# Where the operands of the products lie in SBUF: pads in the tiles and pools of a two-layer trunk

## The chip, the cores and the metric

The kernel runs on 1 core of one Trainium2 chip. The metric is the device time of one execution in microseconds (us). The time before is 1105.18 us, the median of 3 runs (1104.79 to 1105.24).

## What is computed

A trunk of two layers over 512 tokens of 1024 channels, float32. Cut to what matters here:

```
for l in range(2):
    u = rms_norm(h, norm1_g[l]);  proj = u @ w_in[l]              # 1024 x 2576
    mix = concat(pool_mixer(...), diff_attention(...), gla_mixer(...))   # each from slices of proj
    h = h + mix @ w_out[l]                                        # 1024 x 1024
    z = rms_norm(h, norm2_g[l])
    h = h + square(relu(z @ w_mlp1[l])) @ w_mlp2[l]               # 1024 x 4096, 4096 x 1024
return rms_norm(h, final_norm_g)
```

Nearly all of the arithmetic is in these products of matrices.

## The kernel before

Channels lie on the 128 partitions and tokens along the free side. Each large product is made from three products of float32r: both factors are split into a high and a low part (ScalarE casts the high part, VectorE subtracts it to leave the low part; `split`, L118), and high x high, high x low and low x high are added up in one PSUM bank (`mm3`, L138; the page shows them as lines L139 to L141). One such part is one instruction on TensorE, called a product below: it loads 128x128 stationary weights (the page's PEld) and streams the moving operand past them, 512 or 256 columns of 128 partitions (the page's PE).

The order in which names stand in the page: in `psm<-sh,wh` the moving operand is `sh`, the weights are `wh`, and the result goes to `psm`. The stages, each once per layer, in order of time:

- **Projections** (`project`, L330): 512-column products with the normed input `uh`, `ul` moving and a cut weight tile `wh`, `wl` stationary. They are filled in between the steps of the attention and of the gated linear attention (GLA), whose products are small.
- **Values** (`bytoken`, L341): 384 products of 256 columns over both layers, lines L349 to L351. Here the cut weight tile moves and `uh`, `ul` are stationary. GLA's own values are 192 products of 272 columns through the same lines.
- **Output projection** (`output`, L578): 512-column products with `yh`, `yl` or `y` moving.
- **Plain half of the first MLP** (`plain`, L822): 192 products of 512 columns, `zh`, `zl` moving.
- **Seven products** (`seven`, L901): the rest of the first MLP, 28 blocks over both layers by Strassen's scheme with seven smaller products, 84 instructions of 256 columns each, 2352 in all (lines L913 to L915). The moving operand is a quarter of `zh`, `zl` or one of the sums `th1` to `th4`, `tl1` to `tl4`; the weights are `wh`, `wl` (the tile from `cut`) or the sums `bh`, `bl`, `ch`, `cl`, `dh`, `dl` that `prepare` (L881) makes.
- **Second MLP** (`second`, L1003): 1488 products of 512 columns, `sh`, `sl` moving and `wh`, `wl` stationary, and 96 of 256 columns at the very end. Four quarters per layer; each quarter is one stage of seven products and then one of second products.

TensorE's order is the program's own (`manual_schedule`). Weights come by DMA from SyncE's queue, two raw tiles deep, cut tiles three deep. All tiles live in pools (`tile_pool`) that lie one behind the other in SBUF: first `cst`, `res` (h, uh, ul, zh, zl), `wp` (raw, wh, wl), `sm`, and behind these per layer either `at` and `a2` (the attention) or `mp` and `sp` (the MLP). The size of each tile decides where the next one starts. Read from the built program, the places where operands begin, as the start address modulo 128 bytes, are these before and after the change:

| products | columns, count | moving / weights before | apart | moving / weights after | apart |
|---|---|---|---|---|---|
| projections, plain half (`uh` or `zh` with `wh`) | 512, 864 | 32 / 32 | 0 | 32 / 32 | 0 |
| second MLP (`sh` with `wh`) | 512, 1488 | 96 / 32 | 64 | 32 / 32 | 0 |
| seven: `zh` with `wh` | 256, 336 | 32 / 32 | 0 | 32 / 96 | 64 |
| seven: `th1`, `th2`, `th3` with `bh`, `ch` | 256, 1008 | 96 / 96 | 0 | 32 / 96 | 64 |
| seven: `zh` with `ch`, `dh` | 256, 672 | 32 / 96 | 64 | 32 / 96 | 64 |
| seven: `th4` with `wh` | 256, 336 | 96 / 32 | 64 | 32 / 96 | 64 |
| values (`wh` moving, `uh` stationary) | 256, 384 | 32 / 32 | 0 | 96 / 32 | 64 |
| GLA's values, first and third 272 columns of a tile | 272, 120 | 32 / 32 | 0 | 96 / 32 | 64 |
| GLA's values, second 272 columns of a tile | 272, 72 | 96 / 32 | 64 | 32 / 32 | 0 |
| output, `yh` with `wh` or with a spare tile `wx` | 512, 240 | 96 / 32 or 96 | 64 or 0 | 96 / 32 | 64 |
| output, `y` with `wh` or with a spare tile `wx` | 512, 144 | 0 or 96 / 32 or 96 | 0 to 96 | 32 / 32 | 0 |

The low parts lie as the high ones do. The small float32 products of the attention and of GLA (572 of the 6472 instructions) move too; three kinds of transposes among them, with the constants `cn` moving, have their operands 32 (L480), 96 (L519) and 0 bytes (L676) apart before. On VectorE, all operands of `wl<-raw,wh` begin at 32, while in `s<-raw,raw` (L888) they begin at 96, 32 and 96. A step from one 128-column slice of a tile to the next is 512 bytes, so all slices of a tile have its place, but for the 272 columns.

Of the kernel before, what the change touches and what calls it, by code (L numbers as in the profile page):

```python
# [8 lines left out]
F32 = mybir.dt.float32  # L9
F32R = mybir.dt.float32r  # L10
# [6 lines left out]
P = 128  # L17
# [3 lines left out]
KT = D // P  # L21
# [5 lines left out]
NCH = T // CHUNK  # L27
# [6 lines left out]
PLAIN = 2  # L34
HT = T // 2
W = 16 + T
BIG = 1.0e30

LEAD = [(0, 0), (1, 0), (2, 0), (3, 0), (0, 1), (1, 1), (2, 1), (3, 1), (4, 0), (5, 0), (6, 0), (7, 0), (4, 1), (5, 1), (6, 1), (7, 1)]
# [32 lines left out]
def trunk(ctx: ExitStack, tc: tile.TileContext, xt, wfm, wdv, wgv, wout, wm1, wm2, poolw, wg2, par, con, msk, out, outt):  # L72
# [5 lines left out]
    wp = ctx.enter_context(tc.tile_pool(name="wp", bufs=3))  # L78
# [6 lines left out]
    def load(src, n=1024):  # L85
        raw = wp.tile([P, 1024], F32, name="raw", bufs=2)[:, 0:n]
        nc.sync.dma_start(out=raw, in_=src)
        return raw
# [36 lines left out]
            nc.vector.scalar_tensor_tensor(out=dst_l, in0=src, scalar=scale, in1=dst_h.bitcast(F32),  # L125
                                           op0=ALU.mult, op1=ALU.subtract)

    def cut(raw):
        n = raw.shape[1]
        wh = wp.tile([P, 1024], F32R, name="wh")[:, 0:n]  # L130
        wl = wp.tile([P, 1024], F32R, name="wl")[:, 0:n]
        split(wh, wl, raw)
        return wh, wl

    def weights(src, n=1024):
        return cut(load(src, n))

    def mm3(ps, sh, sl, mh, ml, first, last):  # L138
        nc.tensor.matmul(ps, sh, mh, start=first, stop=False)  # L139
# [98 lines left out]
    for l in range(L):  # L238
# [4 lines left out]
        lead = []  # L243
# [3 lines left out]
        for k in range(KT):  # L247
            for i, m, a, b in LOADS if l == 0 else ():
                if i == k:
                    if a == 0:  # L250
                        lead.append([wp.tile([P, 1024], F32R, name=n) for n in ("wh", "wl")])
                    split(lead[m][0][:, a:b], lead[m][1][:, a:b], first[m][:, a:b])
            split(uh[k], ul[k], h[k], g1[k])
        if l == 0:
# [5 lines left out]
        with ExitStack() as ph:  # L260
            at = ph.enter_context(tc.tile_pool(name=f"at{l}", bufs=1))
# [4 lines left out]
            def mixed(k):  # L266

                if yh[k] is None:
                    y = at.tile([P, 2, T], F32R, name="y", tag=f"Y{k}")
                    yh[k], yl[k] = y[:, 0], y[:, 1]  # L270
                return yh[k], yl[k]

            def tmp(name):
                return a2.tile([P, W], F32, name=name, tag="w", bufs=4)[:, 0:T]
# [7 lines left out]
            def advance():  # L282

                n = sum(len(j["src"]) for j in live)
                for j in todo:
                    if j["w"] is None and j["into"]:
                        if "w" + j["name"][1:] in held:
                            break
                        wh, wl = j["into"]()
                        split(wh, wl, load(j["src"][0]))  # L290
                        j["w"] = [(wh, wl)]
                    elif j["w"] is None:
                        n += len(j["src"])
                        if n > 3:
                            break
                        j["w"] = [weights(x, x.shape[1]) for x in j["src"]]
                        live.append(j)

            def run(j):
# [298 lines left out]
            for x in ORDER:  # L598
                if x in ("v0", "v1"):
                    n = int(x[1])  # L600
# [55 lines left out]
            nc.scalar.activation(ed, ed, AF.Exp)  # L656
            nc.scalar.activation(en, bc, AF.Exp, scale=-1.0)
            nc.scalar.activation(ep, bc, AF.Exp)
            dec = at.tile([P, NCH], F32, name="dec")
            nc.scalar.activation(dec, bc3[:, :, CHUNK - 1], AF.Exp)  # L660
            nc.vector.tensor_tensor(out=ed, in0=kd, in1=ed, op=ALU.mult)
            nc.vector.tensor_tensor(out=ki, in0=kd, in1=en, op=ALU.mult)
# [19 lines left out]
            for half in range(2):  # L682
                n = 4 - half
# [21 lines left out]
            po = pc.tile([P, NT, 256], F32, name="pog", tag="pc")  # L705
            for t in range(NT):
# [7 lines left out]
                for j in range(2):  # L714
                    c = 2 * t + j
# [49 lines left out]
            for u in range(nu):  # L765
                f = SF[u]
# [47 lines left out]
        with ExitStack() as ph:  # L814
            mp = ph.enter_context(tc.tile_pool(name=f"mp{l}", bufs=2))
            byhand = ExitStack()
            byhand.enter_context(tc.manual_schedule(engines={mybir.EngineType.PE}))
            fast = ExitStack()
            sp = fast.enter_context(tc.tile_pool(name=f"sp{l}", bufs=1))
            acts, tz = {}, {}  # L820

            def plain(u, j):  # L822
# [58 lines left out]
            def prepare(u):  # L881

                raw1 = load(wm1[l, u, 0])
                raw2 = sp.tile([P, 1024], F32, name="raw2", bufs=2)
                nc.sync.dma_start(out=raw2, in_=wm1[l, u, 1])
                a = cut(raw1)
                s13 = sp.tile([P, 2, 512], F32, name="s13")
                nc.vector.tensor_tensor(out=s13, in0=raw1.rearrange("p (a b) -> p a b", a=2),  # L888
                                        in1=raw2[:, 0:512].unsqueeze(1).broadcast_to([P, 2, 512]), op=ALU.add)
                b = [sp.tile([P, 2, 512], F32R, name=f"b{n}", bufs=2) for n in "hl"]  # L890
                split(*b, s13)
                s24 = sp.tile([P, 2, 512], F32, name="s24")
                nc.vector.tensor_add(s24[:, 0], s13[:, 1], raw1[:, 0:512])
                nc.vector.tensor_add(s24[:, 1], s24[:, 0], raw2[:, 512:1024])
                c = [sp.tile([P, 2, 512], F32R, name=f"c{n}") for n in "hl"]
                split(*c, s24)
                d = [sp.tile([P, 512], F32R, name=f"d{n}", bufs=2) for n in "hl"]
                split(*d, raw2[:, 512:1024])
                return a, b, c, d

# [64 lines left out]
            w, late = None, None  # L965
            for q in range(QT):
                for u in range(q * UQ, (q + 1) * UQ):
                    if u == 0:
# [10 lines left out]
                        w = prepare(PLAIN)  # L979
# [11 lines left out]
                    if not final:  # L991
                        w = prepare(u + 1)
# [22 lines left out]
                lead = []  # L1015
# [18 lines left out]
                        w = prepare((q + 1) * UQ)  # L1034
                byhand.close()
                if ends:
                    w2t = [weights(wm2[l, q, m]) for m in range(KT - 2, KT)]
                    ph.enter_context(tc.manual_schedule(engines={mybir.EngineType.DVE}))
                    for half in range(2):
                        n = slice(half * HT, (half + 1) * HT)  # L1040
# [90 lines left out]
```

## Time and profile before

| | |
|---|---|
| median of 3 runs | 1105.18 us |
| the profiled execution | 1104.88 us |
| its span on the core | 1103.1 us |
| TensorE busy | 1091.8 us (99%), 6472 instructions |
| VectorE busy | 746.9 us (68%) |
| ScalarE busy | 577.4 us (52%) |
| mean granted TensorE clock | 0.996 |

The span runs from the first to the last instruction of the core; 1.8 us of the execution's time lie outside it. A matmul's row in the timeline has a start and a busy time. The busy times of neighbours overlap, since TensorE takes the next product before the last has drained, so what one product costs in a stream is the distance from its start to the next one's start, called pitch below. It is had from the starts of two products and the number between them.

### The profile page before, as it was taken

To read this page: it belongs to the slowest core of one execution; us is meant where nothing else is said; L and a number is where in the kernel's file an instruction comes from. 1 tells how busy PE (TensorE), PEld (TensorE's weight loads), DVE (VectorE), ACT (ScalarE), POOL (GpSimd) and SP (SyncE) were. 2 spreads that over 40 slices of the span, in tenths; PEclk is the share of its full clock that TensorE was granted. 3 is DMA by queue.
4 is the path that set the end of the run, shared out by engine and by line. 5 is a ranking of instruction groups with operands and counts; after the bars stand their busy time and mean duration, and the time that the engine had idled before them with its cause. 6 is when DMAs were issued, how large, how long until landed. Compare 5 with 4: busy or idle time off the path is not lost.

```text
span 1103.1 us, 16249 instructions
## 1 busy us (share of the span) xinstructions
PE 1091.8 (99%) x6472; PEld 963.2 (87%) x6472; DVE 746.9 (68%) x1115; ACT 577.4 (52%) x998; POOL 47.3 (4%) x84
## 2 busy tenths in 40 slices
PE   9999999999999999999999999999999999999997
PEld 7888898888898898898887988887989989989986
DVE  6587873996676676675637688749866666666654
ACT  6526773774265265265434377648733733733742
POOL 3101000000000000000021110000000000000000
PEclk9999999999999999999999999999999999999999
DMA  6322111432322323312222121214232232332222
GB/s 212 96 67 71 64 58 58 154 115 96 115 97 96 115 96 96 115 59 79 91 79 73 61 86 58 93 43 154 93 115 92 100 115 83 109 115 79 76 77 77
DMA packets 32224, 102.76 MB, mean 93 GB/s; under 512 B 3698, under 2 KB 5524, under 8 KB 32148
## 3 DMA queue, kind: packets, MB, share of 16 engines
q1 hardware_dynamic: 31716, 101.17, 28.2%
q8 instruction: 51, 0.84, 0.3%
q10 hardware_dynamic: 432, 0.55, 0.1%
q14 instruction: 25, 0.20, 0.1%
HBM read 99.61 MB, written 2.10 MB: 92 GB/s over the span
## 4 chain that ended last, share of the span: by engine, by line
PE 96%; issue 1%; DVE 1%; DMA 1%; ACT 0%; SPq 0%; POOLq 0%; DVEq 0%; POOL 0%; ACTq 0%
PE psm L141 18%; PE psm L140 18%; PE psm L139 18%; PE psx L913 5%; PE psx L915 5%; PE psx L914 5%; PE psz L915 2%; PE psz L913 2%; PE psz L914 2%; PE psm L349 2%; PE psm L350 2%; PE psm L351 2%; PE po L492 1%; PE psy L913 1%; PE psy L915 1%; PE psy L914 1%
## 5 line engine op out<-in xcount | busy, mean ns | idle before, releaser
L121 ACT CAST wh<-raw 128x1024 fp32r<-128x1024 f32 (+2 forms) x155 | 160.0, 1034 | 292.4 <-PE psm L140 209.7
L122 DVE TENSOR_TENSOR wl<-raw,wh 128x1024 fp32r<-128x1024 f32 (+2 forms) x155 | 185.9, 1201 | 74.2 <-ACT wh L121 73.8
L141 PE MATMUL psm<-sh,wl 128*128 128x512 f32 (+1 forms) x528 | 204.6, 387 | 0.0
L140 PE MATMUL psm<-sl,wh 128*128 128x512 f32 (+1 forms) x528 | 203.3, 385 | 0.0
L139 PE MATMUL psm<-sh,wh 128*128 128x512 f32 (+1 forms) x528 | 201.6, 382 | 0.0
L1011 DVE TENSOR_TENSOR tm<-psm,rb 128x512 f32<-128x512 f32 (+1 forms) x66 | 44.5, 674 | 114.5 <-PE psm L141 114.5
L140 PEld LDWEIGHTS psm<-sl,wh 128*128 128x128 f32 x528 | 99.2, 188 | 21.4
L139 PEld LDWEIGHTS psm<-sh,wh 128*128 128x128 f32 x528 | 99.2, 188 | 20.5
L141 PEld LDWEIGHTS psm<-sh,wl 128*128 128x128 f32 x528 | 99.4, 188 | 18.5
L139 PE MATMUL psm<-uh,wh 128*128 128x512 f32 x224 | 94.8, 423 | 1.4 <-ACT uh L124 1.4
L140 PE MATMUL psm<-ul,wh 128*128 128x512 f32 x224 | 88.5, 395 | 0.3 <-DVE ul L125 0.3
L141 PE MATMUL psm<-uh,wl 128*128 128x512 f32 x224 | 88.6, 396 | 0.1
L349 PE MATMUL psm<-wh,uh 128*128 128x256 f32 (+1 forms) x192 | 56.6, 295 | 0.0
L351 PE MATMUL psm<-wh,ul 128*128 128x256 f32 (+1 forms) x192 | 54.7, 285 | 0.0
L350 PE MATMUL psm<-wl,uh 128*128 128x256 f32 (+1 forms) x192 | 54.7, 285 | 0.0
L141 PEld LDWEIGHTS psm<-uh,wl 128*128 128x128 f32 x224 | 42.5, 190 | 10.4 <-DVE wl L122 1.0
L139 PEld LDWEIGHTS psm<-uh,wh 128*128 128x128 f32 x224 | 42.7, 190 | 10.1 <-ACT uh L124 1.8
L140 PEld LDWEIGHTS psm<-ul,wh 128*128 128x128 f32 x224 | 42.7, 191 | 9.1 <-issue 1.0
L462 ACT ACTIVATE pp<-psc,mn,nrt 128x128 f32<-128x128 f32 (+3 forms) x64 | 39.0, 613 | 13.9 <-DVE mn L459 12.0
L1012 DVE TENSOR_TENSOR h<-h,tm 128x512 f32<-128x512 f32 (+1 forms) x66 | 44.5, 674 | 1.5
L122 DVE TENSOR_TENSOR sl<-o,sh 128x1024 fp32r<-128x1024 f32 (+1 forms) x36 | 35.0, 987 | 11.2 <-ACT sh L121 11.2
L888 DVE TENSOR_TENSOR s<-raw,raw 128x1024 f32<-128x1024 f32 x28 | 34.2, 1222 | 5.8 <-DMA raw<-in_wm 5.5
(381 smaller groups left out, 2727.3 us busy)
## 6 DMA issues: line engine op xcount, KB each, us to landing
raw<-in_wm SPq DMA_DIRECT2D x120, 512.0 KB, 3.5
raw<-in_wfm SPq DMA_DIRECT2D x27, 512.0 KB, 3.5
raw<-in_wout SPq DMA_DIRECT2D x16, 512.0 KB, 3.5
raw<-in_wdv SPq DMA_DIRECT2D x8, 512.0 KB, 3.5
raw<-in_wm SPq DMA_DIRECT2D x16, 256.0 KB, 4.0
h<-in_xt SPq DMA_DIRECT2D x8, 256.0 KB, 5.2
raw<-in_wgv SPq DMA_DIRECT2D x4, 408.0 KB, 3.2
out<-o SPq DMA_DIRECT2D x8, 128.0 KB, 1.8
```

Of the source, the lines that this page charges most:

```text
L121: nc.scalar.copy(out=dst_h, in_=src)
L122: nc.vector.tensor_sub(dst_l, src, dst_h.bitcast(F32))
L139: nc.tensor.matmul(ps, sh, mh, start=first, stop=False)
L140: nc.tensor.matmul(ps, sh, ml, start=False, stop=False)
L141: nc.tensor.matmul(ps, sl, mh, start=False, stop=last)
L349: nc.tensor.matmul(ps, uh[k][:, ts], wh[:, s], start=k == 0, stop=False)
L350: nc.tensor.matmul(ps, uh[k][:, ts], wl[:, s], start=False, stop=False)
L351: nc.tensor.matmul(ps, ul[k][:, ts], wh[:, s], start=False, stop=k == KT - 1)
L913: nc.tensor.matmul(ps, sh[:, s], mh, start=first and k == 0, stop=False, skip_group_check=True)
L914: nc.tensor.matmul(ps, sh[:, s], ml, start=False, stop=False, skip_group_check=True)
L915: nc.tensor.matmul(ps, sl[:, s], mh, start=False, stop=k == 3, skip_group_check=True)
L1011: nc.vector.tensor_tensor(out=tm, in0=ps, in1=r2[:, n], op=ALU.mult)
```

## The change

Tiles and pools get pads. The tiles that hold cut weights are 32 floats (`PAD`, 128 bytes) longer, so that their own places stay, and a view of 16 floats (`HP`, 64 bytes) further in is used where the weights serve 256-column products: `wh`, `wl` in the seven products and the last MLP weights, `b`, `c` and `d`, and the moving weights of the values. An unused tile of 64 bytes at the head of the pool `mp` and one in `at` move all that lies behind them by 64 bytes, and `dec` takes 128 bytes instead of 32. The built programs of before and after have the same instructions in the same order on every engine, with the same waits and the same values waited for; the addresses alone differ.

```diff
+PAD = 32
+HP = PAD // 2
...
-    def cut(raw):
+    def cut(raw, at=0):
         n = raw.shape[1]
-        wh = wp.tile([P, 1024], F32R, name="wh")[:, 0:n]
-        wl = wp.tile([P, 1024], F32R, name="wl")[:, 0:n]
+        wh = wp.tile([P, 1024 + PAD], F32R, name="wh")[:, at:at + n]
+        wl = wp.tile([P, 1024 + PAD], F32R, name="wl")[:, at:at + n]
         split(wh, wl, raw)
         return wh, wl
-    def weights(src, n=1024):
-        return cut(load(src, n))
+    def weights(src, n=1024, at=0):
+        return cut(load(src, n), at)
...
-                        lead.append([wp.tile([P, 1024], F32R, name=n) for n in ("wh", "wl")])
+                        lead.append([wp.tile([P, 1024 + PAD], F32R, name=n)[:, 0:1024] for n in ("wh", "wl")])
...
+            at.tile([P, HP], F32, name="gap")
...
-                        j["w"] = [weights(x, x.shape[1]) for x in j["src"]]
+                        j["w"] = [weights(x, x.shape[1], 0 if j["name"][0] in "po" else HP) for x in j["src"]]
...
-            dec = at.tile([P, NCH], F32, name="dec")
+            dec = at.tile([P, PAD], F32, name="dec")[:, 0:NCH]
...
+            mp.tile([P, HP], F32, name="gap", bufs=1)
...
-                a = cut(raw1)
+                a = cut(raw1, HP)
...
-                b = [sp.tile([P, 2, 512], F32R, name=f"b{n}", bufs=2) for n in "hl"]
+                b = [sp.tile([P, 1024 + PAD], F32R, name=f"b{n}", bufs=2)[:, HP:HP + 1024].rearrange("p (a n) -> p a n", a=2) for n in "hl"]
...
-                c = [sp.tile([P, 2, 512], F32R, name=f"c{n}") for n in "hl"]
+                c = [sp.tile([P, 1024 + PAD], F32R, name=f"c{n}")[:, HP:HP + 1024].rearrange("p (a n) -> p a n", a=2) for n in "hl"]
...
-                d = [sp.tile([P, 512], F32R, name=f"d{n}", bufs=2) for n in "hl"]
+                d = [sp.tile([P, 512 + PAD], F32R, name=f"d{n}", bufs=2)[:, HP:HP + 512] for n in "hl"]
...
-                    w2t = [weights(wm2[l, q, m]) for m in range(KT - 2, KT)]
+                    w2t = [weights(wm2[l, q, m], at=HP) for m in range(KT - 2, KT)]
```

## Rows read from the trace of the kernel before

**Rows 1.** The page: busy time of the engines, and the chain that ended last.
```profile
PE 1091.8 (99%) x6472; PEld 963.2 (87%) x6472; DVE 746.9 (68%) x1115; ACT 577.4 (52%) x998; POOL 47.3 (4%) x84
...
PE 96%; issue 1%; DVE 1%; DMA 1%; ACT 0%; SPq 0%; POOLq 0%; DVEq 0%; POOL 0%; ACTq 0%
```

**Rows 2.** Waits of TensorE: us in total, times, longest; its longest two.
```profile
PE psm L139 <- ACT uh L124: 1.4, 1, 1.4
PE early L112 <- DVE ones L109: 1.0, 1, 1.0
```

**Rows 3.** Windows: stretch, its length, busy us of each engine, clock, DMA share, GB/s.
```profile
256.00:299.70 43.70, 43.70 (x194) 35.88 (x193) 28.93 (x35) 14.23 (x17) 0.00 (x0) 1.00 0.36 116
299.70:339.20 39.50, 39.50 (x338) 39.42 (x337) 26.41 (x34) 25.68 (x41) 0.00 (x0) 1.00 0.25 86
...
76.00:90.00 14.00, 14.00 (x115) 13.85 (x114) 8.51 (x17) 3.52 (x6) 2.91 (x1) 1.00 0.14 39
90.00:158.00 68.00, 68.00 (x398) 59.50 (x397) 56.66 (x121) 53.22 (x127) 4.10 (x6) 1.00 0.22 70
```

**Rows 4.** Timeline of TensorE: start, busy us; first of each run of twelve products.
```profile
311.21 0.28 PE L913 MATMUL psx<-th,wh 128*128 128x256 f32 x1
...
312.57 0.28 PE L913 MATMUL psx<-th,ch 128*128 128x256 f32 x1
...
314.01 0.29 PE L913 MATMUL psy<-zh,dh 128*128 128x256 f32 x1
...
315.39 0.28 PE L913 MATMUL psz<-zh,ch 128*128 128x256 f32 x1
...
316.75 0.28 PE L913 MATMUL psx<-th,bh 128*128 128x256 f32 x1
```

**Rows 5.** Groups of instructions, shapes apart: busy us, mean ns of one; 256 columns.
```profile
L913 PE MATMUL psx<-th,ch 128*128 128x256 f32 x112 | 31.7, 283 | 0.0
...
L913 PE MATMUL psx<-zh,wh 128*128 128x256 f32 x112 | 31.6, 282 | 0.0
...
L913 PE MATMUL psz<-zh,ch 128*128 128x256 f32 x112 | 31.0, 277 | 0.0
...
L913 PE MATMUL psx<-th,wh 128*128 128x256 f32 x112 | 30.9, 276 | 0.0
```

**Rows 6.** Timeline of TensorE: ends of a plain run, of a second and a seven stage.
```profile
230.75 0.39 PE L139 MATMUL psm<-zh,wh 128*128 128x512 f32 x1
...
236.19 0.28 PE L913 MATMUL psx<-zh,wh 128*128 128x256 f32 x1
...
255.95 0.39 PE L139 MATMUL psm<-sh,wh 128*128 128x512 f32 x1
...
299.90 0.28 PE L913 MATMUL psx<-zh,wh 128*128 128x256 f32 x1
...
339.28 0.39 PE L139 MATMUL psm<-sh,wh 128*128 128x512 f32 x1
```

**Rows 7.** Groups in 299.8 to 339.2 us alone: the one group that holds a stall.
```profile
L913 PE MATMUL psx<-th,bh 128*128 128x256 f32 x16 | 4.6, 288 | 0.0
...
L915 PE MATMUL psx<-th,bl 128*128 128x256 f32 x16 | 4.5, 282 | 0.0
```

**Rows 8.** Timeline of TensorE: first and tenth plain product after another stage.
```profile
212.56 0.39 PE L139 MATMUL psm<-zh,wh 128*128 128x512 f32 x1
...
214.65 0.39 PE L139 MATMUL psm<-zh,wh 128*128 128x512 f32 x1
```

**Rows 9.** Timeline of TensorE: two value products, 24 products apart.
```profile
80.95 0.28 PE L349 MATMUL psm<-wh,uh 128*128 128x256 f32 x1
...
83.82 0.28 PE L349 MATMUL psm<-wh,uh 128*128 128x256 f32 x1
```

**Rows 10.** Groups of TensorE, shapes apart: GLA values, transposes, output projection.
```profile
L350 PE MATMUL psm<-wl,uh 128*128 128x272 f32 x64 | 18.5, 289 | 0.0
L480 PE MATMUL ptr<-cn,pp 128*128 128x128 f32 x80 | 14.0, 272 | 1.0 <-DVE y L125 1.0
L140 PE MATMUL psm<-y,wh 128*128 128x512 f32 x30 | 11.9, 397 | 0.0
...
L519 PE MATMUL ptd<-cn,od 128*128 128x128 f32 x32 | 4.8, 272 | 0.0
...
L676 PE MATMUL pk<-cn,edqd 128*128 128x128 f32 x8 | 1.2, 272 | 0.0
```

**Rows 11.** Groups of VectorE, shapes apart: busy us, mean ns of one.
```profile
L122 DVE TENSOR_TENSOR wl<-raw,wh 128x1024 fp32r<-128x1024 f32 x147 | 179.0, 1220 | 66.3 <-ACT wh L121 65.9
...
L888 DVE TENSOR_TENSOR s<-raw,raw 128x1024 f32<-128x1024 f32 x28 | 34.2, 1222 | 5.8 <-DMA raw<-in_wm 5.5
```

## The prediction

> **What bounds the kernel now.** I read the page first. TensorE is busy for 1091.8 us, 99% of the span, and the chain that ended last is TensorE for 96% [rows 1]. The list of waits then says whether it ever stands still: the longest wait of TensorE is 1.4 us, once, the next 1.0 us, both at the start [rows 2]. The windows of the stages show the same from the other side: in a stage of second products (256.0 to 299.7 us) and in one of seven products (299.7 to 339.2 us) TensorE is busy for the whole window at the full clock, 1.00 (2.4 GHz), while VectorE has 28.9 of 43.7 us and 26.4 of 39.5 us, ScalarE 14.2 and 25.7 us, and the DMA engines a share of 0.36 and 0.25 [rows 3]. So the time is the sum of the pitches of TensorE's products, and an edit that changes no instruction can act only through the pitch. I therefore looked for products alike in shape and role but with different places of their operands.
>
> 256 columns. In one block of seven the run `th,wh`, whose operands are 64 bytes apart, takes 311.21 to 312.57 us: 1.36 us for 12 products, 113.3 ns each. The next run, `th,ch`, 0 apart, takes until 314.01: 1.44 us, 120.0 ns. Then `zh,dh`, 64 apart: 1.38 us, 115.0 ns, and `zh,ch`, 64 apart: 1.36 us, 113.3 ns [rows 4]. Over the whole run the mean busy times say it again: 283 and 282 ns for `th,ch` and `zh,wh`, both 0 apart, 277 and 276 ns for `zh,ch` and `th,wh`, both 64 apart [rows 5]. The same moving tile is quick with one weight tile and slow with the other, and the same weight tile likewise. It is the distance that goes with the pitch, not either place alone: 32 with 32 and 96 with 96 are slow, 32 with 96 and 96 with 32 are quick.
>
> 512 columns. The second MLP, 64 apart, takes 255.95 to 299.90 us for 192 products: 228.9 ns each. The last run of the plain half, 0 apart, takes 230.75 to 236.19 us for 24: 226.7 ns [rows 6]. Here 0 is the quicker place, by 2.2 ns.
>
> By the Trainium skill, "TensorE: Matmul & The Clock Gate", sections "Step-by-step: what each phase is for" and "Back-to-back issue gap", TensorE reads the moving operand and the weights through two independent ports that don't take bandwidth from each other, and a warm product follows the last after its columns divided by 2.4 GHz plus some 2.5 ns. An estimate from that page is 109.2 ns at 256 columns and 215.8 ns at 512, wherever the operands lie; the trace shows 113.3 and 120.0 ns, and 226.7 and 228.9 ns, so it agrees with neither the figure nor the independence, and by the rule the change would bring nothing (the third rival).
>
> **The change part by part.** The sum is made against the profiled execution, 1104.88 us (span 1103.1 us), which is 0.30 us under the median.
>
> *Seven products.* All 2352 come to lie 64 apart; 1344 of them were 0 apart. A stage of 336 takes 299.90 to 339.28 us, 39.38 us [rows 6]. One stall is in it that no place explains: `th,bh` in `psx` has 288 ns on line L913 and 282 on L915, 6 ns x 16 = 0.10 us [rows 7]. Without it, 39.28 us / 336 = 116.9 ns. For the pitch after I take 113.4 ns: two runs give 113.3 [rows 4], and the 120.0 ns run less the difference of 6 to 7 ns in mean busy time [rows 5] gives 113 to 114, which are the bounds. (116.9 - 113.4) x 2352 = 8.2 us, with bounds of 6.8 and 9.2. The stall stays.
>
> *Second MLP.* 1488 products go from 64 apart to 0, and then have the very places of the plain half, 32 and 32. 228.9 - 226.7 = 2.2 ns x 1488 = 3.3 us. Against this stands the entry: after another stage the first nine plain products took 212.56 to 214.65 us, 2.09 us [rows 8], where nine at 226.7 are 2.04. Eight entries x 0.05 = 0.4 us; the present stage has nothing of it in its mean that I could take off. Net 2.9 us. The worst bound is that the products stay as slow as in the entry: 2.09 us / 9 = 232.2 ns, a loss of 3.3 x 1488 = 4.9 us.
>
> *Values.* 384 products go from 0 to 64 apart. They take 80.95 to 83.82 us for 24, 119.6 ns [rows 9], and I take the same 113.4 after, though there the weights move and `uh` stands still: 6.2 x 384 = 2.4 us, bounds 0 and 2.5.
>
> *The rest.* Of the 272-column products 120 go to 64 and 72 to 0; they have 289 ns [rows 10], and no row shows the places of the two apart. At 7 ns the net 48 are 0.3 us either way; I take nothing. In the output projection 144 `y` products come to 0 apart; the group that I show has 397 ns [rows 10], against 392 for a product at 228.9 (the distance from pitch to busy time at 256 columns is 283 - 120 = 163 ns), so at most 8 ns x 144 = 1.1 us, at least nothing; 60 `yh` products go from 0 to 64, a loss of 0.1 us. I take a gain of 0.3 us together. The 572 float32 instructions move too, but transposes that lie 32, 96 and 0 apart have 272 ns each [rows 10]: nothing, at 1 ns each 0.6 us either way. VectorE and ScalarE also read and write at the new places. VectorE's 1024-column subtraction takes 1220 ns with all operands at one place, and the sum of the same size 1222 ns with one operand 64 from the others [rows 11]: no cost.
>
> *What is late next.* Where TensorE gets shorter, VectorE would have to go from 26.4 us to over 38 us in a seven stage to bind [rows 3], so nothing there. The tightest stretch is the attention, where VectorE has 56.7 and ScalarE 53.2 of 68 us; the values are filled in there and in GLA, where the engines are far from full (8.5 of 14 us) but stand in a chain of dependent steps [rows 3].
>
> Sum: 8.2 + 2.9 + 2.4 + 0.3 = 13.8 us, 1104.88 - 13.8 = 1091.1 us.
>
> **The rivals.** First, 512 columns bring nothing. For it: 2.2 ns is small, the comparison is between two stages with other work beside them, and both places differ, 96 and 32 against 32 and 32. Against it: the places after are word for word those of the plain half. Time: 1104.88 - 8.2 - 2.4 - 0.3 = 1094.0 us; with the worst bound above, 1098.9.
>
> Second, the shorter products uncover waits. The values cover GLA's and the attention's dependent steps; if all that they save is waited away, and each of the eight seven stages stalls longer by what one run of twelve saves (12 x 6.6 ns = 0.08 us, 0.6 us in all), 3.0 us of the 13.8 are lost: 1094.1 us. For it: the stall of rows 7 shows that such an edge is there. Against it: waits of any length are almost absent now [rows 2].
>
> Third, no effect: the two kinds of twelve products differ by something else that goes with the tile, and the change doesn't do what it says. All four combinations of places in rows 4 and 5 speak against it. Time 1104.9 us. This is what the rule quoted from the Trainium skill would give.
>
> Fourth, slower. A switch from one pair of tiles to another starts a slow phase: `zh,dh` at 115.0 against 113.3 ns behind a switch [rows 4], the nine entry products at 232.2 against 226.7 [rows 8]. If at the new places that phase held on instead of dying out, the seven products would stand at the 120.0 ns of `th,ch`, (120.0 - 116.9) x 2352 = 7.3 us more, and the second MLP 4.9 us more: 1117.1 us. A slow product costs 3.1 ns and a quick one saves 3.5, so it decides once over half of them stay slow. Against it: behind `zh,dh` the very next run is at 113.3, and the 24 plain products hold 226.7.
>
> **How the numbers follow.** Forecast 0.68, first rival 0.10, second 0.15, third 0.04, fourth 0.03. The forecast's own bounds: 9.2 instead of 8.2, 2.5 for 2.4, 1.4 of the rest (1.1 and 0.3) for 0.3, the entry's 0.4 not paid, give 1088.5; 6.8 instead of 8.2 gives 1092.5. The first two rivals reach to 1094.1, and what lies between the first and its worst bound is taken in to 1096. The range is 1088.6 to 1096 us; left out are the third and fourth rival and part of the first. No change is within 0.2%, 2.2 us, about what a measurement of this kernel can tell. Faster by more: the forecast and the first two rivals, 0.93. Same: 0.04. Slower: 0.03.
>
> **What would show it.** In the profile after, all 256-column groups of the seven and of the values have a mean of 276 to 277 ns, but the one with the stall; the second MLP's three lines, now spread, come together at 389 to 390 ns, as the plain half's; a seven stage takes 38.2 us and a second stage 43.6 us. TensorE's list of waits stays as short as it is, and VectorE's 1024-column groups stay at 1220 ns. I am wrong if a 256-column group stays at 282 ns or above with its operands 64 apart, if the second stage is not under 43.9 us, or if new waits of TensorE add up to over 2 us.

## The result and the profile after

The changed kernel takes 1113.32 us (median of 4 runs, 1112.96 to 1114.19), the kernel before 1105.21 us in the same session: a ratio of 1.0077, interval 1.0065 to 1.0089. It is slower by 8.1 us where I forecast 13.8 us less, and it lies outside my range. The profiled execution has 1114.19 us (span 1112.4) against 1104.88 (span 1103.1), 9.3 us more.

The page of the changed kernel, busy time of the engines and the chain that ended last:

```profile
PE 1100.6 (99%) x6472; PEld 963.8 (87%) x6472; DVE 747.3 (67%) x1115; ACT 577.0 (52%) x998; POOL 47.4 (4%) x84
...
PE 96%; issue 1%; DVE 1%; DMA 1%; ACT 0%; SPq 0%; DVEq 0%; POOLq 0%; POOL 0%; ACTq 0%
```

TensorE is the bound as before [rows 1], with the same 6472 instructions, and is busy for 8.8 us longer. VectorE, ScalarE and GpSimd stay within 0.4 us. The waits of TensorE after (line, what it waited for: us in total, times, longest) are no longer than they were [rows 2]:

```profile
PE early L115 <- DVE ones L112: 1.0, 1, 1.0
PE ptr L485 <- DVE y L128: 1.0, 2, 0.5
PE psm L142 <- ACT uh L127: 1.0, 1, 1.0
```

So the products themselves got slower. The groups of TensorE, shapes apart (busy us, mean ns of one): first the second MLP and the plain half before, then the same and the 256-column groups after. Lines L142 to L144 are L139 to L141 of before, L919 is L913:

```profile
L141 PE MATMUL psm<-sh,wl 128*128 128x512 f32 x496 | 195.5, 394 | 0.0
L140 PE MATMUL psm<-sl,wh 128*128 128x512 f32 x496 | 194.5, 392 | 0.0
L139 PE MATMUL psm<-sh,wh 128*128 128x512 f32 x496 | 192.5, 388 | 0.0
...
L141 PE MATMUL psm<-zh,wl 128*128 128x512 f32 x64 | 25.0, 391 | 0.0
L140 PE MATMUL psm<-zl,wh 128*128 128x512 f32 x64 | 25.0, 390 | 0.0
```

```profile
L144 PE MATMUL psm<-sh,wl 128*128 128x512 f32 x496 | 197.1, 397 | 0.0
L143 PE MATMUL psm<-sl,wh 128*128 128x512 f32 x496 | 196.1, 395 | 0.0
L142 PE MATMUL psm<-sh,wh 128*128 128x512 f32 x496 | 194.6, 392 | 0.0
...
L919 PE MATMUL psz<-zh,ch 128*128 128x256 f32 x112 | 31.2, 279 | 0.0
...
L919 PE MATMUL psx<-th,wh 128*128 128x256 f32 x112 | 31.2, 278 | 0.0
...
L919 PE MATMUL psx<-zh,wh 128*128 128x256 f32 x112 | 31.1, 278 | 0.0
...
L919 PE MATMUL psx<-th,ch 128*128 128x256 f32 x112 | 31.0, 277 | 0.0
...
L144 PE MATMUL psm<-zh,wl 128*128 128x512 f32 x64 | 25.4, 396 | 0.0
L143 PE MATMUL psm<-zl,wh 128*128 128x512 f32 x64 | 25.3, 395 | 0.0
```

Two things stand here. The second MLP's three lines, which should have come together at 389 to 390 ns, are at 392 to 397 (388 to 394 before). The plain half's products, which the change was to leave alone, are at 395 and 396 (390 and 391 before). At 256 columns `th,ch` and `zh,wh` did get shorter, from 283 and 282 to 277 and 278 ns, and `zh,ch` and `th,wh` longer, from 277 and 276 to 279 and 278 [rows 5]: the short and the long met in the middle.

The timeline of TensorE after (start, busy us) at the edges of the stages answers to [rows 6]:

```profile
256.87 0.39 PE L142 MATMUL psm<-sh,wh 128*128 128x512 f32 x1
...
301.54 0.28 PE L919 MATMUL psx<-zh,wh 128*128 128x256 f32 x1
...
341.00 0.39 PE L142 MATMUL psm<-sh,wh 128*128 128x512 f32 x1
```

A second stage takes 44.67 us for 192 products, 232.7 ns each (228.9 before). A seven stage takes 39.46 us for 336 (39.38 before). The windows of these stages after (stretch, length, busy us of TensorE, its weight loads, VectorE, ScalarE, GpSimd, clock, DMA share, GB/s) show nothing else that could be the cause. TensorE is busy throughout at the full clock, the other engines have the load that they had [rows 3]:

```profile
256.87:301.54 44.67, 44.67 (x195) 36.16 (x194) 29.08 (x36) 14.26 (x18) 0.00 (x0) 1.00 0.38 115
301.54:341.00 39.46, 39.46 (x338) 39.38 (x336) 26.35 (x34) 25.61 (x41) 0.00 (x0) 1.00 0.25 84
```

If I add up, kind by kind, the distances from each product's start to the next start on TensorE in the two traces, I get where the 9.3 us come from (us, each rounded by itself):

| products | before | after | change |
|---|---|---|---|
| second MLP, 512 columns | 340.6 | 346.5 | +5.9 |
| its last products, 256 columns | 12.1 | 12.2 | +0.1 |
| projections into the blocks | 165.2 | 166.8 | +1.6 |
| output projection | 91.2 | 92.2 | +1.0 |
| plain half of the first MLP | 44.7 | 45.5 | +0.8 |
| seven products | 275.8 | 276.4 | +0.6 |
| values | 47.0 | 46.3 | -0.7 |
| all others | 118.7 | 118.6 | -0.1 |
| sum | 1095.4 | 1104.6 | +9.3 |

All 512-column products lose, the seven products gain nothing, and of the terms that I forecast only the values went that way.

### The profile page after: what moved, and what is told of

It is laid out like the page before. It is cut to its first block, busy times and chain, and to the rows that moved or that the text cites. A ratio compares the mean times of both kernels' runs of the same rounds, so it can differ in the third digit from the quotient of the medians.

```text
span 1112.4 us, 16249 instructions
## 1 busy us (share of the span) xinstructions
PE 1100.6 (99%) x6472; PEld 963.8 (87%) x6472; DVE 747.3 (67%) x1115; ACT 577.0 (52%) x998; POOL 47.4 (4%) x84
## 4 chain that ended last, share of the span: by engine, by line
PE 96%; issue 1%; DVE 1%; DMA 1%; ACT 0%; SPq 0%; DVEq 0%; POOLq 0%; POOL 0%; ACTq 0%
PE psm L144 18%; PE psm L143 18%; PE psm L142 18%; PE psx L919 5%; PE psx L920 5%; PE psx L921 5%; PE psz L920 2%; PE psz L919 2%; PE psz L921 2%; PE psm L354 2%; PE psm L355 2%; PE psm L356 2%; PE po L497 1%; PE psy L920 1%; PE psy L919 1%; PE psy L921 1%
## 5 line engine op out<-in xcount | busy, mean ns | idle before, releaser
L144 PE MATMUL psm<-sh,wl 128*128 128x512 f32 (+1 forms) x528 | 206.2, 390 | 0.0
L142 PE MATMUL psm<-sh,wh 128*128 128x512 f32 (+1 forms) x528 | 203.7, 386 | 0.0
L142 PEld LDWEIGHTS psm<-sh,wh 128*128 128x128 f32 x528 | 99.8, 189 | 21.9
L144 PEld LDWEIGHTS psm<-sh,wl 128*128 128x128 f32 x528 | 99.1, 188 | 21.2
L142 PE MATMUL psm<-uh,wh 128*128 128x512 f32 x224 | 94.8, 423 | 1.0 <-ACT uh L127 1.0
L144 PE MATMUL psm<-uh,wl 128*128 128x512 f32 x224 | 89.5, 399 | 0.2
L142 PEld LDWEIGHTS psm<-uh,wh 128*128 128x128 f32 x224 | 43.0, 192 | 10.3 <-ACT uh L127 1.4
L144 PEld LDWEIGHTS psm<-uh,wl 128*128 128x128 f32 x224 | 42.5, 190 | 10.5 <-DVE wl L125 1.0
```

Source lines behind the costliest of these rows:

```text
L144: nc.tensor.matmul(ps, sl, mh, start=False, stop=last)
```

## The experiments

Reading the addresses again gave the theory. A tile of weights was 4096 bytes long, and with the pad it is 4224. The kernel before keeps the high and the low tile of a pair of weights, and the buffers of each, at whole multiples of 256 bytes from each other, so the two tiles of a pair always stand at one place modulo 256. With pads of 128 bytes the low tile is 128 off. Modulo 128 that can't be seen; modulo 256 the high and the low tile part. The theory: the place that counts is the distance between weights and moving operand modulo 256 bytes, for the high and the low weights each. The rivals were that the pads or the new places cost something in another way, that the places of the moving tiles do it, and that the entry into a stage does it. Below, a pair such as (64, 192) is the distance of the high and of the low weights from the moving operand modulo 256; the pitch is the distance of starts in the trace, in ns.

**The pads alone, at two sizes.** `pad128` is the kernel before with longer `wh` and `wl` and no view moved; `pad512` has pads of 512 bytes.

```diff
+PAD = 32
...
-        wh = wp.tile([P, 1024], F32R, name="wh")[:, 0:n]
-        wl = wp.tile([P, 1024], F32R, name="wl")[:, 0:n]
+        wh = wp.tile([P, 1024 + PAD], F32R, name="wh")[:, 0:n]
+        wl = wp.tile([P, 1024 + PAD], F32R, name="wl")[:, 0:n]
```

(`pad512`: `PAD = 128`.)

> The kernel before with nothing but 128 bytes more on each wh and wl tile; no view is moved and no other tile padded. Every operand keeps its place modulo 128. Theory A (what counts is the distance modulo 256 or more, and the 128-byte pads put the high and the low weights 128 bytes apart modulo 256): the products with wh, wl as weights change though nothing moves modulo 128; the second MLP goes from 228.9 to 231 ns or above (at 233, 1488 x 4 ns = 6 us), projections and plain half from 227.7 to 231, in all 4 to 9 us slower: 1109 to 1114 us. Rival B (only the distance modulo 128 counts, and the changed kernel's loss comes from the places of sh, th, b, c, d and from the views): no change, 1105.2 us within 0.2%.

> The same with pads of 512 bytes. All operands keep their places modulo 512. Theory A: no change, 1105.2 us, second MLP 228.9 ns. Rival C (the pads themselves cost, by longer tiles or more SBUF, whatever their size): as slow as with pads of 128 bytes, above 1109 us.

`pad128` took 1112.63 us, 1.0071 times the kernel before (1.0054 to 1.0088). `pad512` took 1104.91, 0.9999 times (0.9990 to 1.0008). Groups of TensorE in `pad128`, and then in `pad512`:

```profile
L140 PE MATMUL psm<-sh,wh 128*128 128x512 f32 x496 | 196.4, 396 | 0.0
L141 PE MATMUL psm<-sl,wh 128*128 128x512 f32 x496 | 195.9, 395 | 0.0
L142 PE MATMUL psm<-sh,wl 128*128 128x512 f32 x496 | 195.4, 394 | 0.0
...
L142 PE MATMUL psm<-zh,wl 128*128 128x512 f32 x64 | 25.4, 397 | 0.0
L141 PE MATMUL psm<-zl,wh 128*128 128x512 f32 x64 | 25.3, 396 | 0.0
```

```profile
L142 PE MATMUL psm<-sh,wl 128*128 128x512 f32 x496 | 195.7, 394 | 0.0
L141 PE MATMUL psm<-sl,wh 128*128 128x512 f32 x496 | 194.5, 392 | 0.0
L140 PE MATMUL psm<-sh,wh 128*128 128x512 f32 x496 | 192.7, 389 | 0.0
```

Pads of 128 bytes on these two tiles, with every place modulo 128 as it was, bring 7.5 us, nearly as much as the whole change lost. Pads four times as long bring nothing: the second MLP's mean pitch is 232.4 with the one and 228.9 with the other, as before. So it is no cost of longer tiles, and the period is longer than 128 bytes.

**The period by itself.** `dist` has no trunk in it (it, `grid`, `history` and `moving` were executed once each, and their pitches are read from that one trace), only groups of 36 products, high weights with both moving tiles and low weights with the high one, as in the kernel. Both weights stand at a distance `d`, in steps of 32 bytes.

```diff
+    for n in (256, 512):
+        for d in range(0, 1024, 32):
+            wh = buf[:, 2048 + d // 4:2048 + d // 4 + P]
+            wl = buf[:, 4096 + d // 4:4096 + d // 4 + P]
+            for i in range(12):
+                nc.tensor.matmul(ps, wh, mh[:, 0:n], start=i == 0, stop=False)
+                nc.tensor.matmul(ps, wh, ml[:, 0:n], start=False, stop=False)
+                nc.tensor.matmul(ps, wl, mh[:, 0:n], start=False, stop=i == 11)
```

> Only products, no trunk: 36 per group, each as in the trunk (high x high, high x low, low x high), with the high and the low weights at the same distance from the moving operand, 0 to 992 bytes in steps of 32, at 256 and then at 512 columns. The output is not the trunk's. Theory A: the pitch repeats with the distance every 512 bytes or every 256, with 0 at 120 ns and 64, 192, 448 at 113 ns for 256 columns, and 0 at 227, 448 at 229 ns for 512 columns. Rival B: it repeats every 128 bytes, so 0, 128, 256 and 384 are alike.

The timeline of TensorE in `dist` (start, busy us), first products of six groups of 512 columns, at `d` of 32, 64, 192, 224, 256 and 288:

```profile
156.91 0.39 PE L92 MATMUL ps<-buf 128*128 128x512 f32 x1
...
165.30 0.40 PE L92 MATMUL ps<-buf 128*128 128x512 f32 x1
...
198.88 0.39 PE L92 MATMUL ps<-buf 128*128 128x512 f32 x1
...
207.12 0.40 PE L92 MATMUL ps<-buf 128*128 128x512 f32 x1
...
215.52 0.39 PE L92 MATMUL ps<-buf 128*128 128x512 f32 x1
...
223.69 0.39 PE L92 MATMUL ps<-buf 128*128 128x512 f32 x1
```

The group at 32 takes 8.39 us / 36 = 233.1 ns, that at 192 8.24 us, 228.9, and that at 256 8.17 us, 226.9. Without the first products of a group the table is (mean pitch of the last nine, and the same again 256 bytes on):

| `d` | 0 | 32 | 64 | 96 | 128 | 160 | 192 | 224 | 256 | 320 | 448 |
|---|---|---|---|---|---|---|---|---|---|---|---|
| 512 columns | 226.7 | 233.6 | 233.6 | 233.9 | 233.3 | 233.3 | 228.9 | 233.0 | 226.7 | 233.6 | 228.9 |
| 256 columns | | 118.6 | 113.3 | 120.0 | 118.6 | 119.6 | 117.8 | 117.8 | 120.0 | 117.8 | 117.8 |

(At 256 columns the group at 0 is the first work of the kernel, with 213 ns a product, and is left out; at 256, 512 and 768 it has 120.0. At 96 the later groups have 117.3 and 117.4.) At 512 columns the period is 256 to within 0.1 ns. The kernel's second MLP, which I called "64 apart", was at 192. Had it been at 64, it would have shown 233.6 and not 228.9. At 256 columns there is a riddle: 64 gives 113.3 once, and 117.8 at 320, 576 and 832. The 113 that I expected at 192 and 448 isn't there either.

**High and low weights apart.** `grid` is `dist` with the two distances chosen separately, in steps of 64 bytes.

```diff
-        for d in range(0, 1024, 32):
+        for dh, dl in [(x, y) for x in range(0, 512, 64) for y in range(0, 512, 64)]:
```

> Only products, 30 per group, with the high weights at 0 to 448 bytes in steps of 64 from the moving operand and the low weights at each of these likewise, 64 pairs at 256 and then at 512 columns. The output is not the trunk's. Theory A: pairs with unequal distances have other pitches than pairs with equal ones: at 512 columns (0, 128) about 233 ns against 227 at (0, 0); at 256 columns (64, 320) about 118 ns against 113 at (64, 64). Rival B: the pairs (0, 0), (0, 128), (128, 0), (128, 128) are alike, and (64, 64), (64, 192), (64, 320) too.

Mean pitch at 512 columns on the left, at 256 columns on the right. Each is the same to within 0.5 ns 256 bytes on, but for (64, 0) at 512 columns (231.1 to 233.4) and, at 256 columns, (128, 0) (117.6 to 118.8), (192, 0) (116.9 to 118.1) and (128, 192) (117.1 to 120.0):

| high \ low | 0 | 64 | 128 | 192 | | 0 | 64 | 128 | 192 |
|---|---|---|---|---|---|---|---|---|---|
| 0 | 226.7 | 231.1 | 231.0 | 229.2 | | 120.0 | 117.8 | 119.1 | 117.8 |
| 64 | 231.2 | 233.2 | 231.1 | 232.0 | | 117.8 | 117.8 | 118.0 | 113.4 |
| 128 | 233.3 | 230.8 | 231.7 | 233.4 | | 117.6 | 118.7 | 118.8 | 120.0 |
| 192 | 228.8 | 228.9 | 234.0 | 228.9 | | 118.0 | 113.3 | 115.4 | 117.8 |

The changed kernel's second MLP stands at (128, 0) or (0, 128), by the buffer that it gets: 233.3 and 231.0 here, and there 233.4 for 1080 products and 231.5 for 408, 232.9 in the mean. `pad128` fits less well: 1080 of its second MLP's products stand at (192, 64) and take 232.6, where the grid has 228.9. So the pair isn't all that counts at 512 columns; what else does isn't shown. In the grid only (0, 0) is clearly better at 512 columns than (192, 192), where the kernel before had the second MLP. At 256 columns its 113 ns lie at (64, 192) and (192, 64), not at (64, 64).

**The change with pads that keep the period.** `mod256` is the changed kernel with pads of 256 bytes, views 64 bytes in, and gaps of 192: the same 64 and 0 apart as the change meant, but modulo 256. `split128` moves the low weights of the 256-column products 128 bytes further, to (64, 192). `second0` is the kernel before with gaps alone, which bring the second MLP to (0, 0).

```diff
-PAD = 32
-HP = PAD // 2
+PAD = 64
+HP = 16
+GAP = 48
...
-            mp.tile([P, HP], F32, name="gap", bufs=1)
+            mp.tile([P, GAP], F32, name="gap", bufs=1)
```

```diff
+LO = 32
...
-        wl = wp.tile([P, 1024 + PAD], F32R, name="wl")[:, at:at + n]
+        lo = at + LO if at else 0
+        wl = wp.tile([P, 1024 + PAD], F32R, name="wl")[:, lo:lo + n]
```

```diff
+            mp.tile([P, 48], F32, name="gap", bufs=1)
+            sp.tile([P, 16], F32, name="gap2")
```

(The first is `mod256` against the changed kernel, whose `gap` in `at` grows likewise, the second `split128` against `mod256`, where `b`, `c` and `d` are treated alike, the third `second0` against the kernel before.)

> The changed kernel with three numbers different: each padded tile is 256 bytes longer instead of 128, the view still starts 64 bytes in, and the gaps are 192 bytes instead of 64. So the places that the change sought modulo 128 hold modulo 256: all 512-column products but those of yh are 0 apart, all of seven's 64 apart with high and low weights alike, the values 192. Theory A (the loss comes from distances modulo 256 that the 128-byte pads made unequal): the second MLP goes to 226.7 ns, 2.9 us under before, projections and plain half stay as before. For the 256-column products the list of pairs leaves two pitches at 64 apart: at 113.3 ns seven and values save 8.2 + 2.4 us and the time is 1091 us; at 117.8 ns they cost 2 us and save 0.7, and the time is 1103.5 us. Rival B (the loss comes from the shifts, not from the pads' length): slower than before, about 1113 us.

> The same, but where a tile serves 256-column products the view of the low weights starts 128 bytes further in than that of the high ones: 64 apart for the high, 192 for the low weights. 512-column products as in the kernel with 256-byte pads. Theory A with what the list of pairs showed, 113.4 ns for (64, 192) in all four places where it stood: seven's products at 113.4 ns, 1091 to 1092 us, also if equal distances lock at 117.8 ns. Rival: which pitch a run takes depends on how it was entered, not on the pair: then (64, 192) too stands at 117 to 118 ns in a part of the runs, 1096 to 1103 us.

> The kernel before with two gaps alone: 192 bytes at the head of the pool of the MLP, 64 bytes behind it, no padded tile. Only sh, sl move, to 0 apart from wh, wl modulo 256; all of seven stays. Theory A: second MLP 226.7 ns instead of 228.9, 3.3 us less and 0.4 for the entries; the 96 products of 256 columns at the end go from 64 to 0 apart, 0.5 us more: 1102.8 us. Rival B (0 apart isn't the quicker place at 512 columns in this stage): 1105 us or more.

| kernel | us | ratio to before | second MLP, us and ns | seven, us and ns | values, ns |
|---|---|---|---|---|---|
| before | | | 340.6, 228.9 | 275.8, 116.9 | 119.6 |
| `mod256` | 1103.25 | 0.9989 (0.9979 to 0.9998) | 337.5, 226.8 | 277.8, 117.8 | 117.8 |
| `split128` | 1093.95 | 0.9900 (0.9885 to 0.9915) | 337.5, 226.8 | 268.9, 113.6 | 117.5 |
| `second0` | 1101.94 | 0.9972 (0.9960 to 0.9983) | 337.5, 226.8 | 275.7, 116.9 | 119.6 |

(The us hold all distances; the ns at 256 columns leave out the few over 150, which stand where a run ends or TensorE is held up.)

Groups of TensorE in `mod256`, busy us and mean ns of one, first the second MLP and then three of the seven products:

```profile
L143 PE MATMUL psm<-sh,wh 128*128 128x512 f32 x496 | 193.0, 389 | 0.0
L144 PE MATMUL psm<-sl,wh 128*128 128x512 f32 x496 | 193.0, 389 | 0.0
L145 PE MATMUL psm<-sh,wl 128*128 128x512 f32 x496 | 192.9, 389 | 0.0
...
L920 PE MATMUL psx<-th,ch 128*128 128x256 f32 x112 | 31.5, 281 | 0.0
...
L920 PE MATMUL psz<-zh,ch 128*128 128x256 f32 x112 | 31.5, 281 | 0.0
...
L920 PE MATMUL psx<-th,wh 128*128 128x256 f32 x112 | 31.5, 281 | 0.0
```

The 512-column term comes out as forecast in all three: the three lines come together at 389, and 340.6 - 337.5 = 3.1 us are gained against my 2.9. The loss of the changed kernel there is gone. In `second0` only the moving tiles were moved, in `grid` only the weights, and (0, 0) has 226.8 and 226.7 ns: it is the distance that counts there. But in `mod256` the seven products come out at the slow one of the two pitches expected: all their groups are at 281 ns, but for the one that holds the stall. Not one is quick, though `zh,ch` has the very places, high and low, that it had in the kernel before, where it took 277 [rows 5] and 113.3 [rows 4]. With (64, 192) in `split128` they are quick. Even so `split128` stays above the 1091 to 1092 us expected of it: the values stay at 117.5 ns and save 0.8 us, not 2.4, and the seven products save 6.9, not 8.2.

**What a run is entered from.** The riddle of `dist` and the slow `zh,ch` of `mod256` say that a pair alone doesn't settle the pitch. `history`, again products alone, runs 24 products of 256 columns at each of five pairs, after 12 or 21 products at another pair or of 512 columns.

```diff
+    C = ((0, 0), (64, 64), (192, 192), (64, 192), (192, 64))
...
+    for first in (4, 7):
+        for d in C:
+            for x in C:
+                if x != d:
+                    group(256, x, first)
+                    group(256, d, 8)
+            group(512, (0, 0), first)
+            group(256, d, 8)
```

> Only products: 24 of 256 columns at each of five pairs of distances (high, low weights), each entered from each of the others and from 512-column products at 0 apart, after 12 and after 21 products. The output is not the trunk's. If the pair alone sets the pitch, each pair has one pitch whatever stood before. If a run locks by how it was entered, (64, 64) and (192, 192) stand at 113.3 ns after some and at 117.8 ns after others; (0, 0) at 119 to 120 always; (64, 192) at 113.3 always, if it has one lock only.

The timeline of TensorE in `history`: the first product of the 24 at (64, 64) and the first behind them, after (0, 0) and then after (64, 192):

```profile
45.40 0.28 PE L94 MATMUL ps<-buf 128*128 128x256 f32 x1
...
48.23 0.28 PE L94 MATMUL ps<-buf 128*128 128x256 f32 x1
...
53.73 0.28 PE L94 MATMUL ps<-buf 128*128 128x256 f32 x1
...
56.45 0.28 PE L94 MATMUL ps<-buf 128*128 128x256 f32 x1
```

The same 24 products with operands at the same places take 2.83 us, 117.9 ns, and 2.72 us, 113.3. In full (the last nine; 12 and 21 products ahead give the same):

| pair | after (0, 0) | after 512 columns | after the other pairs |
|---|---|---|---|
| (0, 0) | 120.0 | 120.0 | 120.0 |
| (64, 64) | 117.8 | 117.8 | 113.3 |
| (192, 192) | 113.3 | 117.8 | 113.3 |
| (64, 192), (192, 64) | 113.3 | 113.3 | 113.3 |

Behind all that stood ahead of them here, runs at the two unequal pairs find 113.3 by themselves, within 6 products. At (0, 0) they stand at 120.0 whatever ran ahead. At (64, 64) and (192, 192) they take one of two pitches by how they are entered, and keep it. The pair ahead doesn't decide alone: the 12 products at (192, 192) that followed (64, 64) at 117.8 stood at 117.6, where the table has 113.3 behind (64, 64) at 113.3. And neither unequal pair was entered from an equal pair at 117.8. In `mod256` every stage comes from 512-column products, so it starts at 117.8, and nothing in it changes that. In the kernel before, a run at (0, 0), `th,ch`, stands ahead of the first run at (64, 64), `zh,dh`. In the isolated groups (64, 64) stays at 117.8 behind (0, 0), but in the kernel `zh,dh` and `zh,ch` reach 113.3 there [rows 4]; why isn't settled. One difference can be read from the built programs: in the kernel before, `th` and `zh` lie at 224 and 160 modulo 256, so that the moving tile changes its place too, and in `history` it never does.

**The phase handed on.** If that is so, the runs of `b`, `c` and `d` can stay at equal places, as long as the run that opens a stage stands at (64, 192). `lock` is `split128` with the low views of `b`, `c` and `d` set back.

```diff
-for n, x in (("h", HP), ("l", HP + LO))]
+for n, x in (("h", HP), ("l", HP))]
```

(On each of the three lines of `b`, `c` and `d`.)

> As the kernel at 1093.95 us, but b, c and d have their high and low parts both 64 bytes from the moving operand again; only wh, wl in seven (672 of 2352 products) and in the values keep the pair (64, 192). If a run at (64, 64) takes over the pitch with which it is entered, as in the history kernel (113.3 ns after (64, 192), 117.8 after 512-column products), the first run of each stage, zh with wh at (64, 192), brings all that follow to 113.3 ns: seven stays at 113.6 ns and the time at 1094 us. If the pair alone sets the pitch, 1680 products stand at 117.8 ns: 7.5 us more, 1101.5 us.

It took 1093.25 us, 0.9897 times the kernel before (0.9881 to 0.9914), the shortest of all, though not to be told from `split128`, and near the 1094 us expected if the phase is handed on; by the pair alone it would have been 1101.5. Its groups of TensorE, and then its timeline at the edges of a second and of a seven stage:

```profile
L922 PE MATMUL psx<-th,ch 128*128 128x256 f32 x112 | 30.9, 276 | 0.0
...
L922 PE MATMUL psy<-zh,dh 128*128 128x256 f32 x112 | 30.9, 276 | 0.0
L922 PE MATMUL psz<-zh,ch 128*128 128x256 f32 x112 | 30.9, 276 | 0.0
```

```profile
254.70 0.40 PE L145 MATMUL psm<-sh,wh 128*128 128x512 f32 x1
...
298.25 0.28 PE L922 MATMUL psx<-zh,wh 128*128 128x256 f32 x1
...
336.57 0.40 PE L145 MATMUL psm<-sh,wh 128*128 128x512 f32 x1
```

`zh,ch` at (64, 64) has 281 ns in `mod256` and 276 here. Between the two kernels only the low tiles `wl` of 256-column products were moved, not those of `c`. The stages take 43.55 and 38.32 us; I had forecast 43.6 and 38.2 for the change.

**The values.** There the weight tile is the moving operand and `uh`, `ul` are stationary, so the places of a high and a low tile can differ on the moving side. `moving` holds the high and the low weights at one place modulo 256 and puts the high and the low moving tile at each of 64 pairs of places, entered from 512 columns.

```diff
+    for dh in range(0, 256, 32):
+        for dl in range(0, 256, 32):
+            group(512, 0, 0, 5)
+            group(256, dh, dl, 8)
```

> Only products: the weights' high and low parts at one place and the moving high and low parts at 0 to 224 bytes before them in steps of 32, 64 pairs, 24 products of 256 columns each, entered every time from 15 of 512 columns at 0 apart, as the values are entered in the trunk. The output is not the trunk's. It is to show why the values stay at 117.4 ns with their moving parts at (192, 64): theory: this pair, entered from 512 columns, has no pitch under 117 ns, and another pair among the 64 has 113.3. If none has, the values' 2.4 us of the forecast could not be had by any place of the weight tiles.

The slowest pairs have 120.2, the quickest 116.7 ns; none comes near the 113.3 that I expected of some pair. So moving the high and the low moving tile against each other doesn't bring the values their 6.2 ns when they are entered from 512 columns. Another entry, a place outside of these 64 pairs or another order of the three products wasn't tried.

## Why the prediction was wrong, step by step

*The bound, and how the change acts.* Right. TensorE is 99% busy after as before, its waits stay as they were, and the time is the sum of the pitches. VectorE's groups didn't move either, as forecast [rows 11]; two of them after, busy us and mean ns of one:

```profile
L125 DVE TENSOR_TENSOR wl<-raw,wh 128x1024 fp32r<-128x1024 f32 x147 | 179.1, 1221 | 67.7 <-ACT wh L124 67.3
...
L894 DVE TENSOR_TENSOR s<-raw,raw 128x1024 f32<-128x1024 f32 x28 | 34.2, 1221 | 5.1 <-DMA raw<-in_wm 5.0
```

*The step that failed* is the sentence "It is the distance that goes with the pitch", with the distances then taken modulo 128, and on it the claim that the second MLP would "have the very places of the plain half, 32 and 32". They were the same places modulo 128 only. My rows could not tell 128 from 256: `th,wh` was at 192 and `zh,ch` at 64, both at 113.3 [rows 4], so 64 and 192 looked like one place, and no row had a pair whose high and low weights lay differently. I compared the operands' starts modulo 128, and did not ask what the tiles' new length does to the second tile of a pair. 4224 is no multiple of 256, and `dist` and `grid` show what follows at 512 columns: 226.7 ns at (0, 0), 231.0 to 233.3 at (128, 0) and (0, 128).

*Seven products*, forecast 8.2 us less, measured 0.6 more. After, four pairs stand side by side; the second half of their runs of twelve is at some 118 ns at (64, 64) and (192, 192), at 113 to 114 for nearly all at (64, 192), and at 119 at (192, 64), but 113.3 in the three of these that open a stage. The two equal pairs stay slow here even behind quick runs at (64, 192), where `history` and `lock` have 113.3, and (192, 64) has 113.3 in `history` and in `pad128`. In the changed kernel `th` lies at 32 and `zh` at 160 modulo 256, in `lock` both at 160; whether this step of the moving tile between the runs keeps them slow wasn't tried, and it is left open. The size of the term was within my bounds of 6.8 to 9.2 where every run was quick: 6.9 us in `split128` and 275.8 - 268.5 = 7.3 in `lock`. What failed is that 64 apart modulo 128 makes a run quick.

*Second MLP*, forecast 2.9 us less, measured 5.9 more; this is past the worst bound that I gave, a loss of 4.9. With the distance made 0 modulo 256 it is 3.1 less, and the entry, for which I had taken off 0.4 us, costs next to nothing in the mean of 226.8.

*Values*, forecast 2.4 us less, measured 0.7. The pitch went from 119.6 to 117.7 and not to 113.4, which I had taken over from products with other operands standing still; in `moving` nothing under 116.7 was found.

*The rest*, forecast 0.3 us less, measured 3.4 more: projections 1.6, output 1.0, plain half 0.8, the second MLP's last products 0.1, all others 0.1 less. I had charged these as if their own places stayed. Their weights sit in the same padded tiles, and so their high and low parts moved apart too.

*The rivals.* The first, 512 columns bring nothing, had the right place to doubt but the wrong price. The second, uncovered waits, hardly shows in the changed kernel, where the seven products got no shorter. It does where they did: in `split128` and `lock` each of the eight stages has, next to the one long distance of some 223 ns that it had before, a second of some 214, 0.8 us in all where that rival had 0.6. The third, no effect, fails: places alone changed the time by +0.8% and by -1.0%. The rule of the Trainium skill behind it ("TensorE: Matmul & The Clock Gate", "Step-by-step: what each phase is for"), two ports that don't disturb each other, would leave the pitch alone; `grid` disagrees, where the pitch of the same products goes from 226.7 to 234.0 ns. The fourth named the nearest thing to what happened, a slow phase that doesn't die out. It is so for equal pairs at 256 columns (117.8 in `mod256`), but it isn't what cost the 5.9 us in the second MLP, and its 1117.1 us came from another sum.

## What to carry to other kernels

Where the time is a sum of product pitches, read the operands' places from the built addresses over a longer period than the one that you think counts, and check every tile that a pad moves along, the second of a pair above all. Two rows that agree with a period of 128 agree with one of 256 as well, so ask for the row that would tell them apart before you trust a period. Here, high and low weights both at 0 modulo 256 from the moving tile serve 512 columns, and (64, 192) for the run that opens a stage serves 256 columns, with the moving tiles of both stages at one place modulo 256; together, in `lock`, they take 1093.25 us, and gaps of 256 bytes in all (`second0`) already give 1101.94.

## What the runs showed of the hardware

The pitch of a product at the full clock depends on where its operands lie: in the fp32r products of these kernels from 226.7 to 234.0 ns at 512 columns and from 113.3 to 120.2 at 256. At 512 columns `dist` shows a period of 256 bytes. The best place differs with the number of columns: (0, 0) is the best at 512 and among the worst at 256. The distance is not all of it: (192, 64) had 228.9 ns in `grid` and 232.6 in `pad128` at 512 columns.

At 256 columns the pitch has a memory. The same 24 products with operands at the same places took 113.3 or 117.8 ns each by what ran ahead of them, and held it to their end; in `mod256` whole stages of 336 products held 117.8. What inside the engine or the memory makes the period and the memory isn't shown by any run here.
